# Mixture of experts: token sums by float32r products of ones, combined inside the next pair, with the next pair's gathering moved forward

## The chip, the cores and the metric

The kernel runs on one core of one Trainium2 chip. The metric is the device time of one execution in microseconds (us), the median of three runs. Everything below is about TensorE (PE), VectorE (DVE), ScalarE (ACT) and the stream of weight loads that SyncE issues; GpSimd does little here.

## The reference, cut to what matters

The program computes two blocks on 256 tokens of width 1024. The change lies wholly in the mixture of experts at the end of the first block. Each token goes to one group of 8 experts and, in it, to 2 of them, so that 32 experts together see 512 rows.

```python
grp_w, grp_idx = lax.top_k(grp_p, 1)
top_w, top_i = lax.top_k(jax.nn.softmax(in_grp, axis=-1), EXPERT_TOP_K)
top_w = top_w / top_w.sum(-1, keepdims=True) * grp_w
combine = jnp.einsum('nk,nke->ne', top_w, jax.nn.one_hot(eid, N_EXPERTS, dtype=jnp.float32))
y = jnp.zeros(t.shape, jnp.float32)
for e in range(N_EXPERTS):
    h = jax.nn.silu(t @ p['w_exp_gate'][e]) * (t @ p['w_exp_up'][e])
    y = y + combine[:, e:e + 1] * (h @ p['w_exp_down'][e])
```

Each expert has two matrices of 1024x512 and one of 512x1024 in float32, 6 MiB, so the 32 experts bring 192 MiB of weights. After it come a layer norm and the second block (a gated MLP and an attention).

## The kernel before

**Pairs.** Experts are taken two at a time: 16 pairs, each one call of `experts`, in a Python loop that is unrolled. An expert has 64 slots for tokens (experts with more would be served in a loop at the end, which this input does not enter). The 128 slots of a pair lie side by side: expert j of the pair (j = 0, 1) has slots 64j to 64j+63 and works on one half of TensorE's columns, so a matmul of expert 0 and one of expert 1 run next to each other.

**A pair step by step.** `choose` builds, on DVE, a 0/1 matrix `gt` (tokens by slots) and a matrix `wt` with the combine weights in place of the ones. `gather(0)` and `gather(1)` multiply the normalised tokens `hn` by `gt` on PE: 8 float32 matmuls each, for four of the eight chunks of 128 features, into a PSUM tile named `tr`. DVE and ACT take turns to move the chunks to `xg` (even chunks L931 on DVE, odd ones L929 on ACT). `wt` is transposed on PE and copied to `wT`. `products(0)` and `products(1)` accumulate `gate` and `up` over the chunks; ACT and DVE form `h = silu(gate) * up` (L969, L970); PE transposes `h` (L973), ACT copies it to `hT` (L975); the down products make `y0` and `y1`, 512 columns each (L984). Then DVE multiplies them by the gate row `gtf` (L989), and PE multiplies `wT` by the result, once for each block of 128 tokens (L992, four float32 matmuls of 512 columns into PSUM tiles named `sc`); DVE adds each to `acc` (L993).

```python
        gather(0)
        if hook:
            ...
        else:
            gather(1)
        choose(wt, 2)
        pw = ps2.tile([128, 2, 128], F32, name="tr", bufs=2)
```

**PSUM.** The pool holds two tiles named `tr`, two named `sc`, and one each of `gate`, `up`, `y0` and `y1`. Gatherings, both kinds of transposes and nothing else use `tr`, in the order of the program, alternately.

**Order.** Each engine works through its instructions in the order written for it. A scheduler sets that order when the kernel is built, from the order of the code and from the waits; `after(x)` asks that what follows is not placed before x. In the build before, the scheduler has taken gathering matmuls of the next pair forward: half of `gather(0)` into the gap before the down products, and from pair 6 on more of them into the midst of the down products.

**Float32 and float32r.** A float32 matmul shows in the trace as two records. The products outside the experts use float32r, a number in two parts (`h` and `l`), with three matmuls of one record each (L185 to L187); the parts come from an ACT cast and a DVE subtraction.

**Weights.** One queue (SyncE, L124) loads tiles of 1 MiB, 12 to a pair, in the order of use, into 23 slots that fall free when the matmuls that read them are done.

Of the kernel before, what the change touches and what calls it, by code (L numbers as in the profile page):

```python
# [26 lines left out]
NE = 32  # L27
# [18 lines left out]
# rows that are spread over the partitions  # L46
# [3 lines left out]
# constants that depend on shapes alone  # L50
# [19 lines left out]
# order of the weight tiles of 1 MB  # L70
# [38 lines left out]
def tile_block(ctx: ExitStack, tc: tile.TileContext, W, pk, rows, ca, cb, cc, xc, x, cv, dec, wr, wst, bst, out):  # L109
# [65 lines left out]
    def split(src, idle=False, ha=None, la=None):  # L175
        """src in two parts. Not before ha and la; idle: VectorE has a norm to finish."""
# [12 lines left out]
    def product_by_tokens(po, name, nt, yh, yl):  # L189
        """yh + yl (features on partitions) times a matrix of 1024 columns; the last tile one token block after the other."""  # L190
# [20 lines left out]
    # ------------------------------------------------------------------ block one  # L211
# [39 lines left out]
    # the rest of the modulation is of the input alone: its columns on partitions, its rows along the free axis  # L251
# [34 lines left out]
    # the order of the memory: what the last round needs no more comes first  # L286
# [8 lines left out]
    # the scales come first: the first products take the scaled input alone, in the place of the context, and the  # L295
    # shift's share is added to them
# [23 lines left out]
    # depthwise convolution  # L320
# [75 lines left out]
    # retention  # L396
# [6 lines left out]
    # log sigmoid of the decays: min(x, 0) - log1p(exp(-|x|)), by the series of atanh  # L403
# [46 lines left out]
    # tokens on partitions: two blocks of x, two of the context  # L450
# [167 lines left out]
    # the rest of the modulation  # L618
# [8 lines left out]
    # side by side: the memory of a split falls free as a whole  # L627
# [7 lines left out]
    # per feature: scale and shift after the first layer norm, half the gate of the mixing, its bias, half the gates' bias  # L635
# [25 lines left out]
    # the router acts on the input of the layer norm: its matrix takes the scale, its sums the mean, its bias the shift  # L661
# [18 lines left out]
    # convolution branch: normalise over channels with tokens on partitions, and back  # L680
# [28 lines left out]
    # the tiles of the experts' weights, in the order in which their memory falls free  # L709
# [13 lines left out]
    # the gates of both branches, as 1 + tanh of half: twice the sigmoid  # L723
# [26 lines left out]
    # merge of the branches and the mixing product  # L750
# [61 lines left out]
    def spread(psum, name, cols, last=None, **kw):  # L812
        """512 features, by partition in cols, along the free axis of all partitions."""
# [15 lines left out]
    # ------------------------------------------------------------------ mixture of experts  # L829
# [9 lines left out]
    # place in the expert's slots, member, weight  # L839
# [42 lines left out]
    def combine_weights():  # L882
        # the two weights: softmax over the groups at its largest, and over the two chosen experts
# [14 lines left out]
        # further rounds of 64 slots: (more than 64) + (more than 128) + (more than 192)  # L898
# [5 lines left out]
    def experts(load, e0, hook=None, base=None):  # L904
        gt = m2.tile([128, 2, 128], F32, name="gt", bufs=1)
        wt = m2.tile([128, 2, 128], F32, name="wt", bufs=1)
        def choose(t, k):
            for b in range(2):
                for j in range(2):
                    e = e0 + j  # L910
# [3 lines left out]
        choose(gt, 1)  # L914
        xg = m2.tile([128, 8, 128], F32, name="xg", bufs=1)
        pgu = []

        def gather(i):
            cuts = 2 if hook else 1
            pg = [ps2.tile([128, 4 // cuts, 128], F32, name="tr", bufs=2) for _ in range(cuts)]  # L920
            pg = [t[:, k, :] for t in pg for k in range(4 // cuts)]
            for k in range(4):
                m = 4 * i + k
                for b in range(2):
                    T.matmul(pg[k], hn[:, b, m * 128:(m + 1) * 128], gt[:, b, :], start=b == 0, stop=b == 1)
# [8 lines left out]
        def products(half):  # L934
            w = [[load(4 * half + 2 * u + j) for j in range(2)] for u in range(2)]
            for u in range(2):
                for k in range(4):
                    c = 4 * half + k
                    for j in range(2):
                        done = T.matmul(pgu[u][64 * j:64 * j + 64, :], xg[:, c, 64 * j:64 * j + 64],  # L940
                                        w[u][j][:, k * 512:(k + 1) * 512], start=c == 0, stop=c == 7,
                                        tile_position=(0, 64 * j))
            return done

        gather(0)
        if hook:
            pgu.extend(ps2.tile([128, 512], F32, name=n) for n in ("gate", "up"))
            lead = low[0]
            done = products(0)
            with after(lead):  # L950
                hook()
# [661 lines left out]
```

## Time and profile before

| what | us |
|---|---|
| median of the 3 runs shown | 1536.93 (1534.96 to 1539.31) |
| profiled execution: span from first to last instruction | 1536.7 |
| PE busy | 1473.9 (96%) |
| DVE busy | 907.7 (59%) |
| ACT busy | 536.7 (35%) |
| loads and stores of queue q1, as a share of 16 DMA engines | 63.5% |

No time of its own is listed for the profiled execution beside its span; the span lies 0.2 us below the median, so the profile stands for the runs. PE's busy share is that of overlapping records and says little by itself: what counts is how far apart the starts of its instructions lie. The clock column of the profile is the share of full speed that TensorE was granted; full speed is 2.4 GHz, and the level below is 1.2 GHz.

### The profile page before, as it was taken

What the parts mean: (1) busy time and instruction counts of PE and PEld (TensorE: products, weight loads), DVE (VectorE), ACT (ScalarE), POOL (GpSimd) and SP (SyncE); (2) the same over time, 40 slices, a digit from 0 to 9 for tenths busy, and PEclk for the clock granted to TensorE, in tenths of its full rate; (3) what the DMA queues carried; (4) which work ended last, traced back from release to release, by engine and by line L of the source; (5) the groups of instructions that cost most, each with busy time, mean ns of one, the idle gap of its engine ahead of it and who ended that gap; (6) DMA issues with size and microseconds to landing.
All of it is one profiled execution on the core that took longest, in us unless ns stands there. A gap on an engine that the chain in (4) does not pass through costs nothing. (4 is left out here: it accounts for less than half of the span.)

```text
span 1536.7 us, 22943 instructions
## 1 busy us (share of the span) xinstructions
PE 1473.9 (96%) x9391; PEld 1091.1 (71%) x9391; DVE 907.7 (59%) x1583; ACT 536.7 (35%) x802; POOL 124.0 (8%) x104
## 2 busy tenths in 40 slices
PE   6989999999999999999999999979999899999997
PEld 4878898989998434343344333348998799999995
DVE  3899999887675422332222322186768556777766
ACT  3846353423563100010001000135444544453643
POOL 0043031200000000000000000030000110111110
PEclk9999999999999999999999999999999999999999
DMA  9862545465777899999999998327553456545540
GB/s 363 321 218 99 189 179 194 158 210 196 317 308 323 313 406 408 408 405 377 384 403 392 393 364 339 138 86 301 190 198 145 154 173 226 197 161 200 170 125 29
DMA packets 60942, 390.37 MB, mean 254 GB/s; under 512 B 7840, under 2 KB 10400, under 8 KB 16800
## 3 DMA queue, kind: packets, MB, share of 16 engines
q1 hardware_dynamic: 55584, 378.37, 63.5%
q10 hardware_dynamic: 5248, 10.49, 2.8%
q8 instruction: 75, 1.23, 0.3%
q14 instruction: 35, 0.29, 0.1%
HBM read 377.29 MB, written 1.05 MB: 246 GB/s over the span
## 5 line engine op out<-in xcount | busy, mean ns | idle before, releaser
L181 DVE TENSOR_TENSOR l_w<-w,h_w 128x1024 fp32r<-128x1024 f32 x228 | 295.6, 1306 | 74.2 <-ACT h_w L179 70.3
L179 ACT CAST h_w<-w 128x1024 fp32r<-128x1024 f32 x232 | 239.3, 1048 | 265.2 <-PE mm L186 144.2
L187 PE MATMUL mm<-xh,l_w 128*128 128x256 f32 x704 | 199.6, 283 | 4.7 <-DVE l_w L181 4.7
L185 PE MATMUL mm<-xh,h_w 128*128 128x256 f32 x704 | 201.4, 286 | 0.0
L186 PE MATMUL mm<-xl,h_w 128*128 128x256 f32 x704 | 199.4, 283 | 0.0
L187 PEld LDWEIGHTS mm<-xh,l_w 128*128 128x128 f32 x704 | 135.3, 192 | 5.1 <-DVE l_w L181 5.1
L185 PEld LDWEIGHTS mm<-xh,h_w 128*128 128x128 f32 x704 | 135.3, 192 | 0.9
L186 PEld LDWEIGHTS mm<-xl,h_w 128*128 128x128 f32 x704 | 135.3, 192 | 0.1
L984 PE MATMUL y<-w,hT 128*64 128x512 f32 x512 | 132.9, 599 | 0.7 <-ACT hT L975 0.7
L940 PE MATMUL gate<-w,xg 128*64 128x512 f32 x512 | 128.7, 596 | 0.0
L940 PE MATMUL up<-w,xg 128*64 128x512 f32 x512 | 126.3, 592 | 0.0
L185 PE MATMUL mm<-uh,h_w 128*128 128x256 f32 (+1 forms) x400 | 121.6, 304 | 2.1 <-ACT h_w L179 2.1
L187 PE MATMUL mm<-uh,l_w 128*128 128x256 f32 (+1 forms) x400 | 119.6, 299 | 2.6 <-DVE l_w L181 2.6
L186 PE MATMUL mm<-ul,h_w 128*128 128x256 f32 (+1 forms) x400 | 119.2, 298 | 0.0
L331 DVE SCALAR_TENSOR_TENSOR cacc<-zp,pka,cacc 128x256 f32<-128x256 f32 x240 | 118.1, 512 | 1.7
L970 DVE TENSOR_TENSOR h<-h,up 128x512 f32<-128x512 f32 x16 | 11.0, 688 | 180.4 <-PE up L940 180.4
L929 ACT ACTIVATE xg<-tr,fv,fv 128x128 f32<-128x128 f32 x64 | 29.3, 458 | 242.2 <-DVE xg L931 242.2
L940 PEld LDWEIGHTS up<-w,xg 128*64 128x64 f32 x512 | 40.2, 137 | 73.2 <-issue 73.2
L984 PEld LDWEIGHTS y<-w,hT 128*64 128x64 f32 x512 | 41.5, 136 | 67.1 <-issue 62.4
L940 PEld LDWEIGHTS gate<-w,xg 128*64 128x64 f32 x512 | 38.1, 137 | 67.0 <-issue 65.5
L187 PE MATMUL mm<-h_w,xl 128*128 128x256 f32 (+1 forms) x256 | 80.0, 313 | 2.7 <-DVE xl L1105 2.7
L185 PE MATMUL mm<-h_w,xh 128*128 128x256 f32 (+1 forms) x256 | 81.9, 320 | 0.0
(406 smaller groups left out, 2870.6 us busy)
## 6 DMA issues: line engine op xcount, KB each, us to landing
w<-in_W_dram SPq DMA_DIRECT2D x343, 1024.0 KB, 7.3
sw<-raw ACTq DMA_DIRECT2D x48, 128.0 KB, 4.6
w<-in_W_dram SPq DMA_DIRECT2D x8, 512.0 KB, 11.7
xt<-in_xc_dram SPq DMA_DIRECT2D x4, 512.0 KB, 6.0
sw<-qk ACTq DMA_DIRECT2D x8, 256.0 KB, 4.5
v<-vt ACTq DMA_DIRECT2D x16, 128.0 KB, 2.4
cbt<-in_cb_dram SPq DMA_DIRECT2D x1, 1152.0 KB, 11.3
ya<-in_W_dram SPq DMA_DIRECT2D x2, 512.0 KB, 10.0
```

The source lines that it names most:

```text
L179: high[:] = [A.copy(h, src)]
L181: low[:] = [(G if idle else V).tensor_tensor(l, src, h.bitcast(F32), op=OP.subtract)]
L185: T.matmul(ps, sh, mh, start=start, stop=False)
L186: T.matmul(ps, sh, ml, start=False, stop=False)
L187: return T.matmul(ps, sl, mh, start=False, stop=stop)
L331: V.scalar_tensor_tensor(cacc[:, m, :], src, pv("dw", m * 31 + t), cacc[:, m, :], op0=OP.mult, op1=OP.add)
L929: A.activation(xg[:, m, :], pg[k], AF.Identity, scale=fA[:, m:m + 1], bias=fB[:, m:m + 1])
L940: done = T.matmul(pgu[u][64 * j:64 * j + 64, :], xg[:, c, 64 * j:64 * j + 64], w[u][j][:, k * 512:(k + 1) * 512], start=c == 0, stop=c == ...
L970: V.tensor_tensor(h, h, pgu[1], op=OP.mult)
L984: T.matmul(py[n][64 * j:64 * j + 64, :], hT[:, c, 64 * j:64 * j + 64], w[j][:, o:o + 512], start=c == 0, stop=c == 3, tile_position=(0, 64 ...
```

## The change

The function `experts` becomes a class `Pair` whose steps are called one by one. Three things differ. First, `wT`, which held the combine weights, becomes `gT`, which holds ones in float32r, and the weight of each slot becomes one column `ws` (a sum over the transposed `wt`). Second, the output of an expert is scaled by `gtf` and `ws` and split in two float32r parts `ysh` (ACT) and `ysl` (DVE), and each of the four sums becomes two matmuls. Third, these sums of pair p (`combine(0)`, `combine(1)`) are called inside the products of pair p+1, and the gathering of pair p+1 inside pair p: `gather(0)` after the up product, `gather(1)` after the transposes of `h`. The first pair and the last differ at the edges. The queue of loads has the same order as before.

```diff
...
-    def experts(load, e0, hook=None, base=None):
...
+    class Pair:
+        def __init__(self, load, e0):
+            self.load, self.e0 = load, e0
+            self.gt = m2.tile([128, 2, 128], F32, name="gt", bufs=1)
+            self.choose(self.gt, 1)
...
-        def gather(i):
-            cuts = 2 if hook else 1
+        def gather(self, i, cuts=1):
+            if i == 0:
+                self.xg = m2.tile([128, 8, 128], F32, name="xg", bufs=1)
+            xg = self.xg
             pg = [ps2.tile([128, 4 // cuts, 128], F32, name="tr", bufs=2) for _ in range(cuts)]
             pg = [t[:, k, :] for t in pg for k in range(4 // cuts)]
...
+        def products(self, half, u):
+            if half == u == 0:
+                self.pgu = [ps2.tile([128, 512], F32, name=n) for n in ("gate", "up")]
+            if u == 0:
+                self.w = [[self.load(4 * half + 2 * v + j) for j in range(2)] for v in range(2)]
+            for k in range(4):
+                c = 4 * half + k
+                for j in range(2):
+                    done = T.matmul(self.pgu[u][64 * j:64 * j + 64, :], self.xg[:, c, 64 * j:64 * j + 64],
+                                    self.w[u][j][:, k * 512:(k + 1) * 512], start=c == 0, stop=c == 7,
+                                    tile_position=(0, 64 * j))
             return done
...
-        else:
-            gather(1)
-        choose(wt, 2)
-        pw = ps2.tile([128, 2, 128], F32, name="tr", bufs=2)
-        for b in range(2):
-            T.transpose(pw[:, b, :], wt[:, b, :], ident)
-        wT = m2.tile([128, 2, 128], F32, name="wT", bufs=1)
-        V.tensor_copy(wT, pw)
...
-        for n in range(2):
+        def weights(self):
+            wt = m2.tile([128, 2, 128], F32, name="wt", bufs=1)
+            self.choose(wt, 2)
+            pw = ps2.tile([128, 2, 128], F32, name="tr", bufs=2)
+            for b in range(2):
+                T.transpose(pw[:, b, :], wt[:, b, :], ident)
+            self.ws = m2.tile([128, 1], F32, name="ws", bufs=1)
+            V.tensor_reduce(self.ws, pw.rearrange("p b t -> p (b t)"), axis=AX.X, op=OP.add)
+            self.gT = m2.tile([128, 2, 128], F32R, name="gT", bufs=1)
+            V.tensor_scalar(self.gT, pw, 0.0, None, op0=OP.is_gt)
+        def act(self):
+            self.h = m2.tile([128, 512], F32, name="h", tag="h", bufs=3)
+            A.activation(self.h, self.pgu[0], AF.Silu)
+            V.tensor_tensor(self.h, self.h, self.pgu[1], op=OP.mult)
+        def turn(self):
+            ph = ps2.tile([128, 4, 128], F32, name="tr", bufs=2)
+            for k in range(4):
+                done = T.transpose(ph[:, k, :], self.h[:, k * 128:(k + 1) * 128], ident)
+            self.hT = m2.tile([128, 4, 128], F32, name="hT", tag="h", bufs=3)
+            A.copy(self.hT, ph)
+            return done
...
+        def combine(self, n):
             ns = slice(n * 512, (n + 1) * 512)
-            ys = m2.tile([128, 512], F32, name="ys", tag="h", bufs=3)
-            V.tensor_tensor(ys, py[n], gtf[:, ns], op=OP.mult)
+            py = self.py[n]
+            V.tensor_tensor(py, py, gtf[:, ns], op=OP.mult)
+            yh, yl = (m2.tile([128, 512], F32R, name=k, tag="h", bufs=3) for k in ("ysh", "ysl"))
+            A.activation(yh, py, AF.Copy, scale=self.ws)
+            V.scalar_tensor_tensor(yl, py, self.ws, yh.bitcast(F32), op0=OP.mult, op1=OP.subtract)
             for b in range(2):
                 pc = ps2.tile([128, 512], F32, name="sc", bufs=2)
-                T.matmul(pc, wT[:, b, :], ys, start=True, stop=True)
+                T.matmul(pc, self.gT[:, b, :], yh, start=True, stop=False)
+                T.matmul(pc, self.gT[:, b, :], yl, start=False, stop=True)
                 adds.append(V.tensor_tensor(acc[0][:, b, ns], acc[0][:, b, ns], pc, op=OP.add))
...
     acc, adds = [], []
+    last_pair, pair = None, Pair(lambda k: tiles[k], 0)
     for p in range(16):
         moe_tiles(12 * p + 12)
-        experts(tiles[12 * p:].__getitem__, 2 * p, *(() if p else (combine_weights, start)))
+        if p == 0:
+            pair.gather(0, 2)
+            lead = low[0]
+            pair.products(0, 0)
+            done = pair.products(0, 1)
+            with after(lead):
+                combine_weights()
+            with after(done):
+                pair.gather(1, 2)
+            pair.weights()
+        else:
+            pair.products(0, 0)
+            done = pair.products(0, 1)
+            with after(done):
+                last_pair.combine(0)
+        done = pair.products(1, 0)
+        if last_pair:
+            with after(done):
+                last_pair.combine(1)
+                pair.weights()
+        else:
+            start()
+        done = pair.products(1, 1)
+        pair.act()
+        if p < 15:
+            next_pair = Pair(lambda k, o=12 * p + 12: tiles[o + k], 2 * p + 2)
+            with after(done):
+                next_pair.gather(0)
+            done = pair.turn()
+            with after(done):
+                next_pair.gather(1)
+        else:
+            pair.turn()
+        pair.down()
+        if p == 15:
+            for n in range(2):
+                pair.combine(n)
+        last_pair, pair = pair, next_pair
...
-                experts(load, 0)
-                old = m2.tile([128, 3, 2, NE], F32, name="old", tag="wT", bufs=1)
+                pair = Pair(load, 0)
...
```

**How the instructions stand.** In the rows below a name before `<-` is what is written, the names behind it are what is read, sizes are partitions by columns, xN counts instructions in a row, and a wait names the engine (or the DMA queue) whose semaphore is waited for. `y_NNNN` are the two tiles `y0` and `y1` of a pair. A place where the change reuses a name has it under another line number.

First, PE from the transposes of `h` to the end of the down products, in the middle of the stretch of pairs, before the change (L925 gathers for the next pair):

```order
L973 MATMUL tr<-cat,h 128x128 x4
L925 MATMUL tr<-gt,hn 128x128 x4
L984 MATMUL y_6283<-w,hT 64x512
L984 MATMUL y_6284<-w,hT 64x512
L984 MATMUL y_6283<-w,hT 64x512 x3
L984 MATMUL y_6284<-w,hT 64x512 x3
L925 MATMUL tr<-gt,hn 128x128 x5
L984 MATMUL y_6283<-w,hT 64x512
L984 MATMUL y_6284<-w,hT 64x512
L925 MATMUL tr<-gt,hn 128x128 x6
L984 MATMUL y_6283<-w,hT 64x512 x3
L984 MATMUL y_6284<-w,hT 64x512 x3
```

And PE at the same place after the change, from the up product on, with the waits (L928 gathers for the next pair):

```order
L945 MATMUL up<-w,xg 64x512 x6
L928 MATMUL tr<-gt,hn 128x128 x8
L970 MATMUL tr<-cat,h 128x128 [waits DVE_49]
L970 MATMUL tr<-cat,h 128x128 x3
L928 MATMUL tr<-gt,hn 128x128 [waits Activation_49]
L928 MATMUL tr<-gt,hn 128x128 x7
L984 MATMUL y_6413<-w,hT 64x512 [waits DMAHW7_49]
L984 MATMUL y_6413<-w,hT 64x512 [waits DMAHW0_49]
L984 MATMUL y_6413<-w,hT 64x512 x2
```

Gathering no longer stands between the down products; all of `gather(0)` stands ahead of the transposes of `h` and all of `gather(1)` behind them, ahead of the down products, and its first matmul waits for ACT.

Second, ACT at the same place before the change, `xg` of a pair, `silu`, the copy of the transposed `h`, and `xg` of the next pair:

```order
L929 ACTIVATE xg<-tr,fv_3734,fv_3733 128x128 [waits DVE_49,Activation_49]
L929 ACTIVATE xg<-tr,fv_3734,fv_3733 128x128 [waits DVE_49] x3
L969 ACTIVATE h<-gate 128x512 [waits PE_49,Activation_49]
L975 COPY hT<-tr 128x512 [waits PE_49]
L929 ACTIVATE xg<-tr,fv_3734,fv_3733 128x128 [waits DVE_49,Activation_49]
```

And ACT there after the change:

```order
L993 ACTIVATE ysh<-y_6257,ws 128x512 [waits DVE_49]
L993 ACTIVATE ysh<-y_6258,ws 128x512 [waits DVE_49,Activation_49]
L964 ACTIVATE h<-gate 128x512 [waits DVE_49,PE_49]
L972 COPY hT<-tr 128x512 [waits DVE_49,PE_49]
L932 ACTIVATE xg<-tr,fv_3734,fv_3733 128x128 [waits DVE_49] x4
```

The copy to `hT` still stands ahead of the `xg` evacuations, but now the first two of those four belong to `gather(0)`, which PE has done before the transposes; the two `ysh` are new.

Third, PE in the first products of a pair after the change, where the sums of the pair before it now stand:

```order
L945 MATMUL gate<-w,xg 64x512 x8
L945 MATMUL up<-w,xg 64x512 x8
L997 MATMUL sc<-ysh,gT 128x512
L998 MATMUL sc<-ysl,gT 128x512
L997 MATMUL sc<-ysh,gT 128x512
L998 MATMUL sc<-ysl,gT 128x512
L945 MATMUL gate<-w,xg 64x512 x8
L997 MATMUL sc<-ysh,gT 128x512
L998 MATMUL sc<-ysl,gT 128x512
L997 MATMUL sc<-ysh,gT 128x512
```

Before the change the four `sc` matmuls (L992) stood behind the down products of their own pair; now there are two groups of four float32r matmuls, behind the first up product and behind the second gate product of the next pair.

## Rows read from the trace of the kernel before

**Rows 1.** Busy time by stretch: PE, PEld, DVE, ACT, POOL, clock, DMA share, GB/s.

```profile
505.00:955.00 450.00, 438.69 (x2016) 183.43 (x2017) 124.56 (x295) 44.40 (x87) 0.00 (x0) 1.00 0.95 389
540.00:560.00 20.00, 19.15 (x86) 7.47 (x83) 4.53 (x7) 1.18 (x2) 0.00 (x0) 1.00 1.01 423
1020.00:1040.00 20.00, 17.28 (x73) 13.59 (x72) 19.07 (x24) 13.05 (x18) 7.36 (x3) 0.91 0.47 171
1260.00:1280.00 20.00, 17.68 (x147) 17.47 (x146) 12.04 (x9) 7.77 (x10) 3.42 (x1) 1.00 0.61 192
```

**Rows 2.** Timeline of PE, pair 14: start, us, what, [idle before].

```profile
947.76 3.65 PE L940 MATMUL gate<-w,xg 128*64 128x512 f32 x16
...
958.11 3.60 PE L940 MATMUL up<-w,xg 128*64 128x512 f32 x16
962.58 0.66 PE L973 MATMUL tr<-cat,h 128*128 128x128 f32 x4 [0.86 <-DVE h L970]
...
964.05 3.70 PE L984 MATMUL y<-w,hT 128*64 128x512 f32 x16
...
975.97 3.89 PE L992 MATMUL sc<-ys,wT 128*128 128x512 f32 x8
...
979.92 0.38 PE L959 MATMUL tr<-cat,wt 128*128 128x128 f32 x2
980.23 3.65 PE L940 MATMUL gate<-w,xg 128*64 128x512 f32 x16
```

**Rows 3.** Timeline of PE, pair 0's end, first gate of pairs 1 and 2.

```profile
516.08 0.60 PE L973 MATMUL tr<-cat,h 128*128 128x128 f32 x4
...
531.02 1.07 PE L940 MATMUL gate<-w,xg 128*64 128x512 f32 x2
...
562.18 1.07 PE L940 MATMUL gate<-w,xg 128*64 128x512 f32 x2
```

**Rows 4.** Timeline of all engines, gathering between pairs 5 and 6.

```profile
684.06 2.84 PE L925 MATMUL tr<-gt,hn 128*128 128x128 f32 x24
...
685.16 0.41 DVE L931 TENSOR_SCALAR xg<-tr,fv,fv 128x128 f32<-128x128 f32 x1 [0.21 <-PE tr L925]
...
686.60 0.46 ACT L929 ACTIVATE xg<-tr,fv,fv 128x128 f32<-128x128 f32 x1 [0.48 <-DVE xg L931]
```

**Rows 5.** Timeline of all engines, end of pair 15.

```profile
995.05 0.66 PE L973 MATMUL tr<-cat,h 128*128 128x128 f32 x4 [0.86 <-DVE h L970]
995.74 0.59 ACT L975 COPY hT<-tr 128x512 f32<-128x512 f32 x1 [4.25 <-PE tr L973]
...
996.38 7.14 PE L984 MATMUL y<-w,hT 128*64 128x512 f32 x32 [0.67 <-ACT hT L975]
...
1003.45 3.89 PE L992 MATMUL sc<-ys,wT 128*128 128x512 f32 x8
...
1006.67 1.38 DVE L993 TENSOR_TENSOR acc<-acc,sc 128x512 f32<-128x512 f32 x2
...
1007.98 1.87 DVE L1030 BATCH_NORM_STATS2 bst<-acc 128x6 f32<-128x512 f32 x3
```

**Rows 6.** Timeline of PE, float32r products of 512 columns at full clock.

```profile
1022.81 0.39 PE L186 MATMUL mm<-l_w,xh 128*128 128x512 f32 x1
1023.03 0.40 PE L187 MATMUL mm<-h_w,xl 128*128 128x512 f32 x1
```

**Rows 7.** Timeline of PE, two idle gaps and what ran after the first.

```profile
1033.22 0.50 PE L187 MATMUL mm<-h_w,xl 128*128 128x512 f32 x1 [2.72 <-DVE xl L1105]
...
1034.49 0.63 PE L185 MATMUL mm<-h_w,xh 128*128 128x512 f32 x1
...
1267.56 0.39 PE L187 MATMUL mm<-xh,l_w 128*128 128x256 f32 x1 [2.32 <-DVE l_w L181]
```

**Rows 8.** Group of the page: a DVE operation with three operands, busy us, mean ns.

```profile
L331 DVE SCALAR_TENSOR_TENSOR cacc<-zp,pka,cacc 128x256 f32<-128x256 f32 x240 | 118.1, 512 | 1.7
```

**Rows 9.** DMA issues, 500 to 955 us: count, KB each, us to landing.

```profile
w<-in_W_dram SPq DMA_DIRECT2D x168, 1024.0 KB, 8.9
```

More of the change, by code (lines that the diff above doesn't have):

```diff
@@ L924, in gather @@
                 for b in range(2):
-                    T.matmul(pg[k], hn[:, b, m * 128:(m + 1) * 128], gt[:, b, :], start=b == 0, stop=b == 1)
+                    T.matmul(pg[k], hn[:, b, m * 128:(m + 1) * 128], self.gt[:, b, :], start=b == 0, stop=b == 1)
             for k in range(4):
@@ L932, in gather @@
                                               op1=OP.add)]
[L934 to L942, printed above, removed]
-            return done
@@ L945, in experts @@
[L945 to L951, printed above, removed]
-            with after(done):
-                gather(1)
-        else:
-            gather(1)
-        choose(wt, 2)
-        pw = ps2.tile([128, 2, 128], F32, name="tr", bufs=2)
-        for b in range(2):
-            T.transpose(pw[:, b, :], wt[:, b, :], ident)
@@ L960, in experts @@
-        wT = m2.tile([128, 2, 128], F32, name="wT", bufs=1)
-        V.tensor_copy(wT, pw)
-        if not hook:
-            pgu.extend(ps2.tile([128, 512], F32, name=n) for n in ("gate", "up"))
-            products(0)
-        products(1)
-        if base:
-            base()
-        h = m2.tile([128, 512], F32, name="h", tag="h", bufs=3)
-        A.activation(h, pgu[0], AF.Silu)
-        V.tensor_tensor(h, h, pgu[1], op=OP.mult)
-        ph = ps2.tile([128, 4, 128], F32, name="tr", bufs=2)
@@ L972, in experts @@
-        for k in range(4):
-            T.transpose(ph[:, k, :], h[:, k * 128:(k + 1) * 128], ident)
-        hT = m2.tile([128, 4, 128], F32, name="hT", tag="h", bufs=3)
-        A.copy(hT, ph)
-        py = [ps2.tile([128, 512], F32, name="y%d" % n) for n in range(2)]
-        for half in range(2):
-            w = [load(8 + 2 * half + j) for j in range(2)]
-            for n in range(2):
-                for k in range(2):
-                    c = 2 * half + k
-                    for j in range(2):
-                        o = k * 1024 + n * 512
-                        T.matmul(py[n][64 * j:64 * j + 64, :], hT[:, c, 64 * j:64 * j + 64], w[j][:, o:o + 512],
-                                 start=c == 0, stop=c == 3, tile_position=(0, 64 * j))
@@ new lines, in down @@
+        def down(self):
+            self.py = [ps2.tile([128, 512], F32, name="y%d" % n) for n in range(2)]
+            for half in range(2):
+                w = [self.load(8 + 2 * half + j) for j in range(2)]
+                for n in range(2):
+                    for k in range(2):
+                        c = 2 * half + k
+                        for j in range(2):
+                            o = k * 1024 + n * 512
+                            T.matmul(self.py[n][64 * j:64 * j + 64, :], self.hT[:, c, 64 * j:64 * j + 64],
+                                     w[j][:, o:o + 512], start=c == 0, stop=c == 3, tile_position=(0, 64 * j))
@@ L1050, in load @@
                     return t
-                experts(load, 0)
-                old = m2.tile([128, 3, 2, NE], F32, name="old", tag="wT", bufs=1)
+                pair = Pair(load, 0)
+                for i in range(2):
+                    pair.gather(i)
+                pair.weights()
+                for half in range(2):
+                    for u in range(2):
+                        pair.products(half, u)
+                pair.act()
+                pair.turn()
+                pair.down()
+                for n in range(2):
+                    pair.combine(n)
+                old = m2.tile([128, 3, 2, NE], F32, name="old", tag="gT", bufs=1)
                 V.tensor_copy(old, prw)
```

11 lines of the change are left out of this document (3 added, 8 removed).

## Prediction

> **What bounds the kernel now.** I first read the busy shares by stretch [rows 1]. Between 505 and 955 us PE is busy for 438.69 of 450 us at clock 1.00, DVE for 124.56 and ACT for 44.40; the loads fill 0.95 of the DMA engines at 389 GB/s. So two things are near their limit, PE and the loads. The list of waits names no load among those that PE waits for in this stretch, so PE sets the pace: SyncE waits for PE to free slots, not the other way round. When the loads run free, as in 540 to 560 us, they move 423 GB/s.
>
> Then I read PE's timeline start by start. An early pair takes 31.16 us from gate to gate (531.02 to 562.18) [rows 3]. A late one takes 32.47 (947.76 to 980.23) [rows 2]; the timeline shows the starts of pairs 7 to 15 at this distance. What a pair holds, from the rows of pair 14: three of the four gate and up products last 10.35 us (947.76 to 958.11), 3.45 each, so all four end at 961.56. PE then idles until 962.58, since DVE must form `h`: 1.02 lost. The transposes and 8 records of gathering fill 1.47 us until the down products (964.05), which with more gathering last 11.92 us (964.05 to 975.97) [rows 2], while pair 15's, undisturbed, last 7.07 (996.38 to 1003.45) [rows 5]. Of the 4.85 between, 22 records of gathering explain 2.6 (24 last 2.84 us [rows 4], 0.118 each); the other 2.2 is what it costs to break the down products up. The sums and what remains of gathering and transposes last 4.26 (975.97 to 980.23).
>
> **The change, step by step.** A pair in the middle, after the change, on PE:
>
> 1. Gate and up products: 4 x 3.45 = 13.8 us, as before.
> 2. Sums: 8 float32r matmuls of 512 columns. The nearest rows are such products in the next block: 0.22 to 0.23 us from start to start [rows 6]. 8 x 0.23 = 1.84. Passing from products on half the columns to products on all and back happens four times; no row isolates it. Bounds: nothing, or 0.2 each, since pair 15's 16 down products last 7.07 with the passage at their end, and at the pace of the gate products (8 in 3.45) would last 6.9. I take the low side, 0.04 each, as part of the 0.2 is the wait for DVE there. Together 2.0. Before, four float32 matmuls stood here with DVE in their way, close to 3.8.
> 3. Transposes of `wt`: 0.31 [rows 2].
> 4. `gather(0)`: 16 records, 1.9, with 0.05 for the start: 1.95. It covers the wait for `h` (1.02 above). If that cover were gone, 1.0 per pair would return.
> 5. Transposes of `h`: 0.45 (of the 1.47 above the 8 records take 0.94; 0.53 is left, and I round it down).
> 6. A new wait. `gather(1)` needs the `tr` tile that `gather(0)` filled (there are two, and the transposes of `h` hold the other), and its order row shows a wait for ACT. ACT stands with the copy to `hT` first. Counted from the end of the up product: `gather(0)` ends at 1.95, the transposes at 2.4. ACT starts `hT` 0.69 after the first transpose and needs 0.59 [rows 5]: 2.64 to 3.23. The evacuation runs strictly in turn, DVE, ACT, DVE, ACT: from 685.16 to 687.06 in the row [rows 4], 1.90, of which 1.4 from ACT's first to ACT's last. DVE's first is done by then (2.1 to 2.5: the row starts it 1.10 after the gathering starts). So ACT's last ends at about 4.65 and `gather(1)` starts at 4.7: PE waits 2.3 us. Behind it on PE stand the down products, whose `hT` has long been there. Bounds: below nothing is excluded, as the order shows the wait; the smallest is 1.4 (if the copy didn't delay ACT), the largest 2.7 (0.1 for each of four handovers more).
> 7. `gather(1)` 1.95 and the down products 7.05, not broken up.
>
> Sum: 13.8 + 2.0 + 0.31 + 1.95 + 0.45 + 2.3 + 1.95 + 7.05 = 29.8 us, against 31.16 and 32.5. For the first four pairs the scheduler puts the next pair's first gate matmul into the wait, 0.43 less: 29.4.
>
> DVE and ACT get more to do: two DVE splits and two ACT copies of 512 columns, and a reduction. The trace of before has no such split. Bounds: 0.69, the time of an addition of 512 columns (1.38 for two [rows 5]), and 1.02, twice that of the nearest operation of this kind on 256 columns, 0.51 [rows 8]; I take 0.7, since both read one tile in PSUM. DVE's 124.56 us over 14 pairs [rows 1], 8.9 each, become some 11 of 29.8. Scaling, copy and split stand behind the down products, about 2.5 us long, and their first reader stands 6.9 us of gate and up products later, which hide them at either bound. Without that cover they would be the chain at the end of pair 15, below. The loads keep their order; the queue moves past nothing.
>
> Now the whole stretch. Pair 0 has the same work up to 516.08 [rows 3] (the spread of `ln1_b` goes from behind the up product to ahead of it); then steps 4 to 7, 13.7 us, lead to 529.8, where pair 1 starts with its first gate matmul done. Four pairs of 29.4: 647.4. Ten of 29.8: pair 15 starts at 945.4. Steps 1 to 3: 961.5. It has no next pair, so it waits for `h` and `hT` as before, 994.0 (980.23 + 13.8) to 996.38, 2.35 [rows 2, 5]; down products 7.07: 970.9. Before, they ended at 1003.45. That is 32.5 us less.
>
> At the end the sums of pair 15 stand bare, with a longer chain: scale, ACT copy, DVE split, sum, and all four statistics behind the additions instead of three. Before, from 1003.45 to the end of the last statistics (1007.98 + 1.87) 6.4 us pass [rows 5]. After: `y1` scaled at 1.0, ACT's copy (0.59 for 512 columns [rows 5]) to 1.65, the split to 2.45, the first addition from 2.6, four of 0.69 to 5.4, four statistics of 0.62 to 7.9: 1.5 more, bounds 0 (additions begin under the down products' end) and 2.5 (splits of 1.02). Left: 31 us, 1505.9.
>
> **What the clock does.** A wait of 2.3 us in every pair raises this question. After a gap of 2.72 us a product of 512 columns reads 0.63 us instead of 0.39 [rows 6, 7], and the granted clock of that stretch of 20 us is 0.91 [rows 1]: it fell from 2.4 to 1.2 GHz for a while, and 0.09 x 20 = 1.8 us were lost, of which a little belongs to an earlier fall. I price a fall at 1.6. After a gap of 2.32 us [rows 7] the clock stays 1.00 [rows 1]. My wait stands at the harmless one, 0.4 below the harmful one. I take two falls in the ten pairs without the extra gate matmul, 3 us in all. Result: 1505.9 + 3 = **1509 us**. The sum is made against the profile's span, 1536.7, which lies 0.2 below the median.
>
> **The rivals.**
>
> *The clock falls in all ten pairs, or in all fifteen*: 16 to 24 us come back, 1522 to 1530. For it: the gap that did it was only 0.4 longer. Against it: the 2.32 one. The Trainium skill ("TensorE: Matmul & The Clock Gate", section "A second HAM failure mode: psum-queue depth-cycling") says that a kernel which waits for PSUM banks in every iteration makes the clock swing between its two levels; by that rule this rival's upper end holds, and the trace has it for one gap and not for the other.
>
> *The loads become the bound.* 168 tiles are issued between 500 and 955 us [rows 9], 176 MB; at 389 GB/s [rows 1] they would need 453 us, at 423 only 417, until 917, while PE by my sum uses the last of them at 967. So loads bind only if they can't exceed some 380 GB/s, with 970 and later; at 360 the last tile comes at 989, the down products end at 993 instead of 971, and the time is 1528. The Trainium skill ("HBM Reference", "Specifications (TRN2)") gives a core an effective 358 GB/s of its pair's memory, and more when it streams alone; the trace agrees with the second part, 423.
>
> *The sums get no cheaper*: eight float32r matmuls that each read two banks of weights take 0.46 instead of 0.23, 1.8 x 15 = 28 back: 1534, no change within 0.3%. Against it: rows 6 have a new stationary operand at each product too [rows 6].
>
> *Slower.* If the same wait reaches 4 us it is longer than the gap that lowered the clock, and each of 15 pairs pays 1.7 + 1.6: 50 us, 1556. It decides from 2.4 us per pair in all on.
>
> *The wait is shorter*: at 1.4 and no fall of the clock, 0.9 x 14 less: 1493; if it were hidden, 1474.
>
> **How the numbers follow.** Forecast (1500 to 1516) 0.55; clock rival 0.25; loads 0.04; no cheaper sums 0.04; slower 0.05; shorter wait 0.07. The range 1495 to 1528 holds the forecast and nearly all of the clock rival. A measurement of this kernel can tell about 0.3%, 4.6 us, from no change. Faster: 0.55 + 0.25 + 0.04 + 0.07 = 0.91; same 0.04; slower 0.05.
>
> **What the profile after would show.** Gate to gate 29.4, then 29.8 us; `sc` matmuls 0.23 apart, eight per pair; PE idle about 2.3 us ahead of `gather(1)`, released by ACT's `xg`; down products 7.05 in one piece; pair 15's end near 971. Wrong it would be if PE waited for loads, if the clock of 530 to 940 us were below 0.97, or if the sums waited for DVE's split.

## The result, and the profile after

The changed kernel takes 1492.78 us (median of 4 runs, 1490.13 to 1495.14), the kernel before 1538.12 us on the same chip (4 runs); the ratio is 0.9704, interval 0.9686 to 0.9722. Two later measurements beside other kernels gave 0.9722 (0.9709 to 0.9735) and 0.9724 (0.9699 to 0.9749). The forecast was 1509, and its range ended at 1495: the direction was right, the gain of 45 us is 1.6 times the predicted 28, and the time lies below the range. The profiled execution took 1494.24 us, with a span of 1492.5.

The busy shares by stretch of the changed kernel, in the columns of [rows 1]:

```profile
505.00:955.00 450.00, 440.58 (x2216) 204.63 (x2213) 157.09 (x362) 67.77 (x125) 0.00 (x0) 1.00 0.98 404
640.00:940.00 300.00, 293.25 (x1487) 139.48 (x1487) 102.63 (x236) 45.68 (x85) 0.00 (x0) 1.00 1.01 420
```

The clock is 1.00 over the whole stage, and the loads now run at 420 GB/s for 300 us on end. In [rows 1] they ran at 389 on the mean: SyncE had to wait for PE to free slots. Now PE uses the 12 tiles of a pair, 1.049 MB each, in 28.7 us, which would be 438 GB/s, so it slowly eats up the lead that the loads have.

One pair on PE's timeline (start, duration, instruction, idle time before it):

```profile
705.63 3.65 PE L945 MATMUL gate<-w,xg 128*64 128x512 f32 x16
709.07 3.65 PE L945 MATMUL up<-w,xg 128*64 128x512 f32 x16
712.65 0.50 PE L997 MATMUL sc<-ysh,gT 128*128 128x512 f32 x1
712.98 0.39 PE L998 MATMUL sc<-ysl,gT 128*128 128x512 f32 x1
713.21 0.40 PE L997 MATMUL sc<-ysh,gT 128*128 128x512 f32 x1
...
713.77 3.65 PE L945 MATMUL gate<-w,xg 128*64 128x512 f32 x16
717.35 0.50 PE L997 MATMUL sc<-ysh,gT 128*128 128x512 f32 x1
...
718.39 0.38 PE L956 MATMUL tr<-cat,wt 128*128 128x128 f32 x2
718.70 3.65 PE L945 MATMUL up<-w,xg 128*64 128x512 f32 x16
722.28 2.05 PE L928 MATMUL tr<-gt,hn 128*128 128x128 f32 x16
724.17 0.60 PE L970 MATMUL tr<-cat,h 128*128 128x128 f32 x4
725.45 2.05 PE L928 MATMUL tr<-gt,hn 128*128 128x128 f32 x16 [0.67 <-ACT hT L972]
727.43 7.14 PE L984 MATMUL y<-w,hT 128*64 128x512 f32 x32
734.35 1.08 PE L945 MATMUL gate<-w,xg 128*64 128x512 f32 x4
```

Gate to gate it is 734.35 - 705.63 = 28.72 us, against 31.16 and 32.5 before [rows 2, 3]. The starts of the other pairs lie 28.7 apart too, those of the first four 29.08. The eight sums follow each other in 0.23 us, the `h` wait is gone, the down products run in one piece (727.43 to 734.35, 6.92). One wait is left, 0.67 us ahead of the second gathering, and its releaser is ACT's copy to `hT` (L972). What DVE and ACT do meanwhile:

```profile
724.37 0.41 DVE L934 TENSOR_SCALAR xg<-tr,fv,fv 128x128 f32<-128x128 f32 x1 [1.19 <-PE tr L928]
724.81 0.59 ACT L972 COPY hT<-tr 128x512 f32<-128x512 f32 x1 [6.71 <-DVE xg L934]
725.29 0.46 ACT L932 ACTIVATE xg<-tr,fv,fv 128x128 f32<-128x128 f32 x1
...
725.79 0.41 DVE L934 TENSOR_SCALAR xg<-tr,fv,fv 128x128 f32<-128x128 f32 x1 [1.00 <-ACT xg L932]
726.23 0.46 ACT L932 ACTIVATE xg<-tr,fv,fv 128x128 f32<-128x128 f32 x1 [0.48 <-DVE xg L934]
```

Here the reader sees the point on which the prediction turned. The evacuation (the copies from `tr` to `xg`) of the first gathering does run strictly in turn, DVE 724.37, ACT 725.29, DVE 725.79, ACT 726.23, and ends at 726.69, 4.4 us after the end of the up product (722.28), where 4.65 was worked out. But the second gathering starts at 725.45, in the midst of it. It can't be waiting for this tile. It starts 0.05 after the copy to `hT` ends (724.81 + 0.59 = 725.40). So the two `tr` tiles are not taken alternately in the order of the program, as the paragraph on PSUM ahead of the prediction says: by these starts the second gathering has the tile of the transposes of `h`. Why the tiles were handed out so when the kernel was built is not shown. The list of waits of PE in the stage names the same releaser (what waits, what releases it: us in total, times, longest):

```profile
PE tr L928 <- ACT hT L972: 7.4, 11, 0.7
```

At the end of pair 15:

```profile
954.25 7.14 PE L984 MATMUL y<-w,hT 128*64 128x512 f32 x32 [0.68 <-ACT hT L972]
...
962.03 0.74 DVE L994 SCALAR_TENSOR_TENSOR ysl<-y,ws,ysh 128x512 fp32r<-128x512 f32 x1
...
966.37 2.46 DVE L1076 BATCH_NORM_STATS2 bst<-acc 128x6 f32<-128x512 f32 x4
```

The down products end at about 961.3; the last statistics end at 968.83, 7.5 us later, against 6.4 before [rows 5].

### The profile page after: what moved, and what is told of

It reads as the page before. It is cut to its first block, busy times and chain, and to the rows that moved or that the text cites. A ratio compares the mean times of both kernels' runs of the same rounds, so it can differ in the third digit from the quotient of the medians.

```text
span 1492.5 us, 23025 instructions
## 1 busy us (share of the span) xinstructions
PE 1437.1 (96%) x9391; PEld 1098.6 (74%) x9391; DVE 931.9 (62%) x1631; ACT 557.2 (37%) x834; POOL 125.1 (8%) x104
## 5 line engine op out<-in xcount | busy, mean ns | idle before, releaser
L999 DVE TENSOR_TENSOR acc<-acc,sc 128x512 f32<-128x512 f32 x64 | 41.1, 684 | 135.6 <-PE sc L998 135.6
L945 PE MATMUL gate<-w,xg 128*64 128x512 f32 x512 | 121.9, 596 | 0.5
L945 PE MATMUL up<-w,xg 128*64 128x512 f32 x512 | 120.0, 595 | 0.0
L984 PE MATMUL y<-w,hT 128*64 128x512 f32 x512 | 113.9, 596 | 0.7 <-ACT hT L972 0.7
L187 PEld LDWEIGHTS mm<-uh,l_w 128*128 128x128 f32 x400 | 76.9, 193 | 7.1 <-DVE l_w L181 3.8
L185 PEld LDWEIGHTS mm<-uh,h_w 128*128 128x128 f32 x400 | 77.1, 193 | 6.7 <-ACT h_w L179 1.9
```

Source lines behind the costliest of these rows:

```text
L185: T.matmul(ps, sh, mh, start=start, stop=False)
L187: return T.matmul(ps, sl, mh, start=False, stop=stop)
L945: done = T.matmul(self.pgu[u][64 * j:64 * j + 64, :], self.xg[:, c, 64 * j:64 * j + 64], self.w[u][j][:, k * 512:(k + 1) * 512], start=c = ...
L984: T.matmul(self.py[n][64 * j:64 * j + 64, :], self.hT[:, c, 64 * j:64 * j + 64], w[j][:, o:o + 512], start=c == 0, stop=c == 3, tile_posit ...
L999: adds.append(V.tensor_tensor(acc[0][:, b, ns], acc[0][:, b, ns], pc, op=OP.add))
```

## The experiments

All are changes of the changed kernel; "gate to gate" is the distance of the same instruction in successive late pairs. Early pairs are the first four or five, in which the scheduler has ordered PE's work in another way; late pairs are the rest.

### The tile for which the second gathering waits

Both gatherings take one tile of their own, the two kinds of transposes another, and the down products stand behind the second gathering (this last keeps the order on PE as it is in the changed kernel).

```diff
-            pg = [ps2.tile([128, 4 // cuts, 128], F32, name="tr", bufs=2) for _ in range(cuts)]
+            pg = [ps2.tile([128, 4 // cuts, 128], F32, name=n, bufs=1) for n in ("ga", "tr")[:cuts]]
...
-            ph = ps2.tile([128, 4, 128], F32, name="tr", bufs=2)
+            ph = ps2.tile([128, 4, 128], F32, name="tr", bufs=1)
```

> The changed kernel (1492.8 us), but both gatherings use one PSUM tile of their own and the two kinds of transposes another, and the down products are held behind the second gathering. Theory: the prediction's wait was right for this arrangement and wrong for the real one, where the second gathering took the tile of the transposes of h and waited for the copy to hT alone. Then PE waits here until ACT's last evacuation of the first gathering, about 2.0 us instead of 0.67 by the rows of the changed kernel, gate to gate 30.0 instead of 28.7 us, and 1512 us in all. If such a wait in each of 15 pairs also lowers the clock, 1.6 us more for each, 1536. Rival: the wait doesn't hang on the tile at all (the evacuation is simply quicker than worked out); then the wait stays 0.7 and the time within 3 us of 1493.

Measured: 1518.11 us (4 runs, 1516.74 to 1520.75), ratio 0.9863 (0.9847 to 0.988). The second gathering of three successive pairs on PE's timeline:

```profile
825.94 2.05 PE L928 MATMUL ga<-gt,hn 128*128 128x128 f32 x16 [1.97 <-ACT xg L932]
...
855.90 3.50 PE L928 MATMUL ga<-gt,hn 128*128 128x128 f32 x16 [1.97 <-ACT xg L932]
...
887.46 2.05 PE L928 MATMUL ga<-gt,hn 128*128 128x128 f32 x16 [1.97 <-ACT xg L932]
```

The wait is 1.97 us in each of the eleven late pairs and its releaser is now ACT's `xg` (L932): for the wait the theory holds to 0.03 us. Without a loss of clock a pair takes 29.96 (825.94 to 855.90). But the gathering that starts at 855.90 takes 3.50 us instead of 2.05, and this pair takes 31.56 (to 887.46). Of the eleven such waits in a row the first three cost nothing more, and then every second one lowers the clock: pairs of 31.6, 30.0, 31.6, 30.0 alternate to the end, four falls in all. The granted clock of the stretches shows it (columns as above):

```profile
640.00:720.00 80.00, 74.08 (x379) 32.64 (x379) 24.97 (x58) 12.29 (x23) 0.00 (x0) 1.00 1.01 420
794.00:825.00 31.00, 29.58 (x142) 13.64 (x142) 9.57 (x23) 4.17 (x8) 0.00 (x0) 0.94 0.99 405
```

So both parts of the forecast's mechanism exist, the wait (1.97, predicted 2.3) and the clock's falls (1.6 each, as priced); they belong to an arrangement that the changed kernel doesn't have. From the first gathering to the end of the last down products this run takes 485.9 us, the changed kernel 463.0. Ten late distances 1.25 longer, four early ones 0.9 longer (29.95 against 29.08) and four falls make 22.5 of these 22.9 us; the rest of the 25 us between the medians lies outside of this stretch.

### The remaining wait, taken away

> The changed kernel with the first gathering cut in two: one half ahead of the transposes of h, the other behind them, while ACT copies hT; the down products are held behind the second gathering, and the next gate product behind it too. Theory: the remaining wait is for the copy to hT alone, and 0.94 us of gathering covers its 0.67; h, which now has half of the cover, costs at most 0.1. Gate to gate 28.1 us in all pairs, and 0.36 less for the four pairs whose first gate product was taken forward: 14 x 0.6 + 4 x 0.36 = 10 us less than the changed kernel, about 1483 us. Rival: ACT's evacuation of the first half now delays the copy to hT by as much, and nothing is gained; 1493 us.

```diff
             with after(done):
-                next_pair.gather(0)
+                next_pair.gather(0, part=0)
             done = pair.turn()
             with after(done):
-                next_pair.gather(1)
+                done = next_pair.gather(0, part=1)
+            with after(done):
+                gathered = next_pair.gather(1)
...
-        pair.down()
+            with after(gathered):
+                pair.down()
```

Measured: 1496.39 us (5 runs, 1493.16 to 1499.38), ratio 0.9723 (0.9708 to 0.9739); the changed kernel beside it, which was to be the measure, gave 1494.77.

> The changed kernel once more, as the measure for the run beside it: 1493 us, gate to gate 28.7 us.

The time is the rival's, as nothing was gained; the mechanism is neither's, as the wait grew. PE's timeline:

```profile
839.04 1.16 PE L931 MATMUL tr<-gt,hn 128*128 128x128 f32 x8
840.03 0.62 PE L974 MATMUL tr<-cat,h 128*128 128x128 f32 x4
841.68 2.94 PE L931 MATMUL tr<-gt,hn 128*128 128x128 f32 x24 [1.04 <-ACT xg L935]
```

The second half goes into the tile whose first half is being read, and PE waits 1.04 us for ACT's `xg`. On ACT this `xg` stands behind the copy to `hT` (840.68 to 841.27) and ends at 841.64: the copy delays the evacuation, and not the other way round, as the rival had it. The cover that I wanted to put into the gap needed itself what ACT was late with. Gate to gate 29.1. (In two early pairs, where the scheduler had put two products of the next pair into this gap, the distance was 28.21.)

The next try leaves the order alone and gives the second gathering another tile: one of those named `sc`, which no sum uses at that time. The down products and the next gate product stand behind it.

```diff
-            pg = [ps2.tile([128, 4 // cuts, 128], F32, name="tr", bufs=2) for _ in range(cuts)]
+            names = [("tr", "sc")[i]] if cuts == 1 else ["tr"] * cuts
+            pg = [ps2.tile([128, 4 // cuts, 128], F32, name=n, bufs=2) for n in names]
```

> The changed kernel with the second gathering in a tile of the pair named sc, which is free at that time, instead of tr; the down products and the next gate product are held behind it. Theory: the wait hung on the tile of the transposes of h alone; with another tile PE goes straight on, gate to gate 28.05 us in all pairs, 14 x 0.67 + 4 x 0.36 = 11 us less than the changed kernel: 1483 us. Rival: PE then waits for hT at the down products, or for xg, by as much: 28.7 us and 1494 us.

> The changed kernel once more, on the chip of the run beside it: 1494 us.

Measured: 1479.79 us (5 runs, 1479.46 to 1481.77), ratio 0.9615 (0.9598 to 0.9633); the changed kernel beside it 1497.67 (1490.91 to 1499.62), ratio 0.9724.

```profile
825.48 2.05 PE L929 MATMUL tr<-gt,hn 128*128 128x128 f32 x16
827.37 0.60 PE L972 MATMUL tr<-cat,h 128*128 128x128 f32 x4
827.81 1.95 PE L929 MATMUL sc<-gt,hn 128*128 128x128 f32 x16
829.69 7.14 PE L986 MATMUL y<-w,hT 128*64 128x512 f32 x32
```

No wait is left in a pair: the second gathering follows the transposes at once, and `hT` is there when the down products come. Gate to gate 27.77 in the late pairs and 27.73 in the first four. That is 0.94 and 1.35 less, somewhat more than the 0.67 of the wait and the 0.36; where the other 0.27 lies I read from the starts: the gathering begins 0.44 behind the transposes instead of 1.28, of which the wait explains 0.67, and its own 16 records take 1.88 instead of 1.98. From the first gathering to the end of the last down products it takes 447.2 us, and the changed kernel 463.0 in each of its three profiles: the other tile is worth 15.7 us. The medians differ by 18, but the five times of the changed kernel beside it are spread over 9 us, so that what goes beyond 15.7 is not shown to come from the tile. The kernel before is 59 us slower than this version.

### What each part is worth

Three kernels undo one part each, one leaves only the moved gathering.

Old sums (float32 with `wT`) in the new places:

```diff
-                T.matmul(pc, self.gT[:, b, :], yh, start=True, stop=False)
-                T.matmul(pc, self.gT[:, b, :], yl, start=False, stop=True)
+                T.matmul(pc, self.wT[:, b, :], ys, start=True, stop=True)
```

> The changed kernel with the old sums: wT and float32 products, one per sum, in the places of the changed kernel. Theory: the float32r products are worth the 3.7 us of four float32 products less the 2.1 of the eight new ones, about 1.6 us per pair; gate to gate 30.3 us, 1517 us in all. Rival: the gain comes from the places alone, and the kind of product is worth nothing: gate to gate 28.7, 1493 us.

1515.33 us (4 runs, 1514.54 to 1517.05), ratio 0.9851 (0.9834 to 0.9867); gate to gate 30.30, as expected. Four records of float32 stand where four of float32r stood, and take until the next product 1.92 and 1.82 us instead of 1.12 and 1.04:

```profile
841.41 1.98 PE L993 MATMUL sc<-ys,wT 128*128 128x512 f32 x4
843.33 3.65 PE L945 MATMUL gate<-w,xg 128*64 128x512 f32 x16
846.91 1.98 PE L993 MATMUL sc<-ys,wT 128*128 128x512 f32 x4
848.73 0.38 PE L956 MATMUL tr<-cat,wt 128*128 128x128 f32 x2
```

Float32r sums behind the down products of their own pair:

```diff
-            with after(done):
-                last_pair.combine(0)
...
-                last_pair.combine(1)
...
-        if p == 15:
-            for n in range(2):
-                pair.combine(n)
+        for n in range(2):
+            pair.combine(n)
```

> The changed kernel with the float32r sums behind the pair's own down products instead of inside the next pair. Theory: PE meets there the chain that pair 15 shows (sums end 4.2 us behind its down products, instead of 2.1 us of work), less what the scheduler fills in from the next gate product: 0.5 to 2 us per pair, gate to gate 29.2 to 30.7, 1500 to 1521 us. Rival: the scheduler covers it wholly with gate products, and two passages between half and all columns are saved; 1490 us.

1526.48 us (4 runs, 1525.96 to 1528.19), ratio 0.9923 (0.9906 to 0.9939); gate to gate 31.50 from pair 6 on (30.07 in the first four). That is 2.8 more than with the sums inside the next pair, above the 0.5 to 2 that I allowed.

```profile
832.85 7.14 PE L984 MATMUL y<-w,hT 128*64 128x512 f32 x32
840.60 0.73 PE L997 MATMUL sc<-ysh,gT 128*128 128x512 f32 x2 [0.61 <-ACT ysh L993]
841.26 1.07 PE L945 MATMUL gate<-w,xg 128*64 128x512 f32 x2
...
843.64 0.47 PE L997 MATMUL sc<-ysh,gT 128*128 128x512 f32 x1 [0.64 <-DVE acc L999]
...
844.81 1.51 PE L945 MATMUL gate<-w,xg 128*64 128x512 f32 x6
```

From the end of the down products (839.8) to the gate product at 844.81 it is 5.0 us, of which two gate records are 0.4 and the sums themselves 2.2. Of the other 2.4, 1.25 are the two listed waits in the chain of scaling, copy, split and addition: 0.61 for ACT's `ysh` and 0.64 for DVE's `acc`. The last 1.1 lie between the records, and the profile names no releaser for them. The scheduler found only two records to fill in.

Gathering called ahead of its own pair's products again:

```diff
+            pair.gather(0)
+            pair.gather(1)
             pair.products(0, 0)
...
-            with after(done):
-                next_pair.gather(0)
-            done = pair.turn()
-            with after(done):
-                next_pair.gather(1)
+            pair.turn()
```

> The changed kernel with the next pair's gathering called ahead of its own products again, so that the scheduler may take it forward as in the kernel before (it stands in the midst of the down products). Theory: the wait for h (1.0 us) and the cost of breaking up the down products (2.2 us) come back, the wait of 0.67 goes: gate to gate 31.2 us, 1528 us in all. Rival: breaking up the down products costs nothing, as its cost before belonged to something else: gate to gate 29.1, 1498 us.

1521.05 us (4 runs, 1520.37 to 1524.03), ratio 0.9891 (0.9874 to 0.9908).

```profile
824.67 3.70 PE L984 MATMUL y<-w,hT 128*64 128x512 f32 x16
828.31 1.38 PE L928 MATMUL tr<-gt,hn 128*128 128x128 f32 x10
...
831.48 1.60 PE L928 MATMUL tr<-gt,hn 128*128 128x128 f32 x12
...
836.59 0.49 PE L928 MATMUL tr<-gt,hn 128*128 128x128 f32 x2
```

In late pairs the scheduler breaks the down products up in this kernel too. They take from 824.67 to 836.59 with 22 records of gathering among them, 11.92, as in [rows 2], and gate to gate is 31.43: in the late pairs the theory holds (31.2). In the first five pairs it leaves them whole, and gate to gate is 29.0, even a little less than the changed kernel's 29.08. So the time is 7 us better than expected; moving the gathering is worth 2.7 us in each late pair and nothing in the first. The cost of breaking up the down products was worked out as 2.2 in the prediction; late against early pairs differ by 2.4 here and by 1.3 in the kernel before (32.5 and 31.16), so no single price for it is shown.

Only the moved gathering: float32 sums at their own pair's end.

> Only the moved gathering is left of the change: float32 sums at the end of their own pair, as in the kernel before. Theory: the float32 sums wait there for one DVE operation alone, hidden under the end of the down products, so weaving is worth little without the float32r split (3.9 us against 3.7): gate to gate 30.5 us, 1518 us. Rival: sums at the own pair's end cost 2.8 us more whatever their kind, as they did with the float32r split; gate to gate 33, 1555 us, no gain over the kernel before.

1515.54 us (4 runs, 1514.37 to 1517.24), ratio 0.9853 (0.9837 to 0.9869); gate to gate 30.44.

```profile
831.19 7.14 PE L982 MATMUL y<-w,hT 128*64 128x512 f32 x32
838.26 3.89 PE L993 MATMUL sc<-ys,wT 128*128 128x512 f32 x8
842.08 3.65 PE L945 MATMUL gate<-w,xg 128*64 128x512 f32 x16
```

The sums stand right behind the down products without a listed wait and take 3.82 us. Weaving them into the next pair (30.30 above) saves 0.14. The moved gathering alone brings 22 of the 45 us (1537.3, the kernel before beside it, to 1515.54).

The gate to gate distances of late pairs make a table:

| gathering forward | sums at own pair's end | sums in the next pair |
|---|---|---|
| float32 | 30.44 | 30.30 |
| float32r in two parts | 31.50 | 28.71 |

With the gathering in its old place it is 32.5 for the kernel before (float32, own end) and 31.43 for float32r in the next pair. Neither float32r alone (+1.1) nor weaving alone (-0.1) brings anything to speak of; together they bring 1.7 in a late pair.

### The next bound

The kernel with the divided gathering, without the sums of pairs 0 to 14:

> The arrangement with the divided gathering, with the sums of pairs 0 to 14 and what scales their outputs left out (the weights are still loaded in the same order). PE's own work falls by 2.2 to 2.5 us per pair, to some 25.8. Theory: the loads are the next bound; 192 tiles at 420 GB/s can't land before about 930 us, so PE begins to wait for loads in the last pairs, the last down products end near 936, and the time is 1463 to 1470 us. Rival: the loads keep up with PE; the last down products end near 917, 1449 us.

1472.2 us (2 runs, 1470.75 and 1473.64), ratio 0.9574 (0.9553 to 0.9595): a little above the theory's 1463 to 1470 and far from the rival's 1449. Gate to gate is 26.84 until 849; then PE waits for loads at the second group of gate products of each pair:

```profile
857.40 3.65 PE L949 MATMUL gate<-w,xg 128*64 128x512 f32 x14 [0.40 <-DMA w<-in_W_dram]
...
887.33 3.65 PE L949 MATMUL gate<-w,xg 128*64 128x512 f32 x14 [1.05 <-DMA w<-in_W_dram]
...
917.19 3.65 PE L949 MATMUL gate<-w,xg 128*64 128x512 f32 x14 [0.99 <-DMA w<-in_W_dram]
```

The last pairs take 29.3, 29.9 and 29.8 us instead of 26.84. 12 tiles of 1.049 MB in 29.92 us are 420.6 GB/s, and this is what the loads move there (last column):

```profile
850.00:925.00 75.00, 70.48 (x331) 30.67 (x328) 9.49 (x28) 6.43 (x13) 0.00 (x0) 1.00 1.01 420
```

The list of waits names only 2.5 us of loads in the three pairs. The rest of the 8.5 us is spread between the records: the up products that follow take 4.68 us from start to end instead of 3.65, without a listed wait. Until 849 us PE ran at 26.84 against the 29.9 of the loads, which the lead of up to 23 slots must have covered.

## Why the prediction was wrong

1. *Gate and up products, 13.8*: with what lies between kinds of product they take 14.18 (7.02 + 3.58 + 3.58, from start to start). The passage from half the columns to all costs 0.14 after each of three products (3.58 against 3.44); I had put the passages at the low end of their bounds. 0.4 too little.
2. *Sums, 2.0*: 2.16 (1.12 + 1.35 less 0.31 for the transposes of `wt`). Right, and the price of 0.23 from the next block's rows holds.
3. *Transposes of `wt`, `gather(0)`, transposes of `h`*: 0.31, 1.89 and 0.61, against 2.71 in sum; 0.1 more. `gather(0)` covers the wait for `h`, as said.
4. *The new wait, 2.3*: **this step failed**. It said that `gather(1)` needs the tile that `gather(0)` filled, since there are two and the transposes of `h` hold the other. It took the other one, that of the transposes, and waits for ACT's copy to `hT` alone: 0.67 us instead of 2.3. The order's row named only ACT, and two kinds of instruction stood on ACT there; I took the later. Where the tiles are arranged as I assumed, the wait is 1.97, so the working was fit for its premise and the premise was wrong. The bounds, 1.4 to 2.7, were drawn round the duration and not round the premise, so 0.67 lay outside them.
5. *`gather(1)` 1.95, down products 7.05 in one piece*: 1.98 and 6.92. Right.

Sum: 28.72 instead of 29.8. Over ten late pairs that is 10.9 us, over the first four (29.08, not 29.4) 1.3. From the first gathering (494.86 before, 498.42 here) to the end of the last down products it is 508.6 us before and 462.9 after, 45.7 less, where 32.5 were predicted; the two sums explain 12.2 of these 13.2, and the last 1.0 is not broken down. In the experiment with the longer wait the pair takes 29.96, close to the forecast 29.8, but by luck: the wait is 0.33 shorter than worked out and the other terms together 0.5 longer.

*The gate product taken forward* was to save 0.43 in each of the first four pairs. They take 0.36 more than the late ones: the two records run from 522.49 to 523.46, longer than the wait of 0.67 that they fill, and the gate and up products that are left take 6.97 (532.36 to 539.33), hardly shorter than the 7.02 of a whole group.

*The clock*: the 3 us for two falls did not come, as no gap of that size exists; the rival with falls in each pair (0.25) needed the longer wait, and the first experiment shows that it would have come in part. The price of a fall held, but judging by the length of the gap did not: 1.97, less than the harmless 2.32, lowered the clock four times in eleven. The Trainium skill ("TensorE: Matmul & The Clock Gate", "A second HAM failure mode: psum-queue depth-cycling") says that the clock swings between its levels in a kernel that cycles through PSUM banks in each iteration and leaves TensorE idle for short times between groups of matmuls. The traces agree in part: the changed kernel with its 0.67 shows no swing, the experiment with 1.97 does, from the fourth such wait on.

*The tail*: predicted 1.5 us longer, measured 1.1 (7.5 against 6.4). The split takes 0.74, near the 0.7 taken.

*The rivals*: the loads did not bind, but the chance of 0.04 looks small now; they are the next bound, as the last experiment shows. The sums got cheaper, so that rival fell. "The wait is shorter" (0.07) came true. Its 1493 for a wait of 1.4 came true by luck, by two errors that cancel in part: a wait of 0.67, and passages of 0.4.

*The rest*: this run came 3.6 us later to the first gathering than the kernel before and gained 3.1 behind the last statistics, where two gaps of 2.32 [rows 7] and 2.40 us became one of 1.37. Nothing of the change lies in these stretches. The other two profiles of the changed kernel come to the first gathering at 497.19 and 495.26 and need the same 463.0 us from there to the last down products, so the stretch of pairs repeats and what lies around it scatters. The 1505.9 of the prediction is 31 under the median, 1536.93, and not under the span, as it says; that is 0.2 us.

## What to carry to other kernels

A wait that an order shows names an engine; ask which of that engine's instructions releases it, through which tile, and price the wait for each of them before choosing one. A product in two cheap parts needs other work that hides the longer chain which makes the parts: here the split alone cost 1.1 us a pair, and with weaving it gained 1.7. A filler in a gap must not need the buffer that caused the gap; here another buffer that was idle at that moment brought 15.7 us, and a new order of the same work none.

## What was not expected of the hardware

The length of a gap alone doesn't tell whether the clock falls. Waits of 1.97 us, in the same place of each pair, lowered it in every second pair from the fourth on and left it in the others, while a gap of 2.32 us left it at 1.00 [rows 1, 7] and one of 2.72 lowered it. Even the same gap does not always do it: in the kernel whose second gathering has an `sc` tile, the same gap that lowered the clock in [rows 7] is 2.71 us long, and the stretch around it stays at 1.00, where it was 0.91 [rows 1]. First the stretch, in the columns of [rows 1], then the gap on PE's timeline:

```profile
970.00:990.00 20.00, 17.29 (x78) 13.95 (x77) 17.67 (x17) 11.50 (x15) 8.47 (x4) 1.00 0.56 209
978.25 0.50 PE L187 MATMUL mm<-h_w,xl 128*128 128x512 f32 x1 [2.71 <-DVE xl L1167]
```

Each fall in the first experiment cost 1.6 us (31.55 against 29.96). Why the falls alternate, and why only from the fourth wait on, stays open.

One core's loads held 420 GB/s for 300 us on end, while PE was busy for 293 of them. At that rate the 12 tiles of a pair take 29.9 us, more than the 28.7 that PE now needs. The changed kernel never waits for a load in this stretch, so its lead must keep the loads off the path.
